# Seven products for eight in a part of each down projection

## The chip, the cores and the metric

The kernel runs on one core of one Trainium2 chip. Its engines work side by side, each through its own queue in order: TensorE (PE) multiplies, VectorE (DVE) and ScalarE (ACT) work element by element, GpSimd (POOL) does small vector work, and SyncE (SP) issues the loads of weights. The metric is the device time of one execution in microseconds (us), as the median over runs. The profile is one further execution, recorded by the hardware profiler.

## The reference, cut to what matters

Two layers work on 256 tokens of width 2048. In each, a mixer (a state-space and gated recurrence in the first, sliding-window attention in the second) is followed by an MLP:

```python
D_MODEL = 2048; SEQ = 256; DEPTH = 2; D_FF = 4 * D_MODEL

def rms_norm(x, gain):
    xf = x.astype(F32)
    y = xf * lax.rsqrt(jnp.mean(xf * xf, axis=-1, keepdims=True) + EPS)
    return (y * gain.astype(F32)).astype(x.dtype)

def squared_relu_mlp(xn, w_up, w_down):
    return jnp.square(jax.nn.relu(xn @ w_up)) @ w_down

def reference(...):
    ...
        h = h + y.astype(h.dtype)
        h = h + squared_relu_mlp(rms_norm(h, mlp_norm[layer]), mlp_w_up[layer], mlp_w_down[layer]).astype(h.dtype)
    return h
```

All is float32. w_up is 2048 x 8192 and w_down 8192 x 2048, in each of the two layers.

## The kernel before

**Products.** A float32 product is made of three products of rounded parts: each operand is split into hi (rounded to the matmul type) and lo (the rest), and hi·hi, hi·lo and lo·hi are added up in PSUM.

**Weights.** All weights of the program are one list of units of 512 KB (`add_units`, lines 79 to 82), used strictly in that order. A down unit is two row tiles of 128 rows by 512 columns, an up unit four row tiles by 256 columns. `emit_dma` (line 92) loads a unit into one of four raw tiles through SP's queue; `emit_split` (line 101) makes hi with a rounding copy on ACT (line 105) and lo with a difference on DVE (line 106), into four buffers each. `advance` (line 110) hands out the next unit and, before that, emits loads up to six units ahead and splits up to three units ahead. A raw tile is free for the unit four places on when its split is done.

**The order on the engines.** The program is written as one stream. A scheduler in the compiler then places the instructions on each engine's queue by its own timeline of them, so that an engine's order can differ from the written one where another instruction was ready first. On the chip each queue runs in the order so found, and semaphores hold an instruction back until its inputs are there.

**The MLP** (`mlp`, line 910) cuts the 8192 hidden columns into four chunks of 2048. `up(c)` makes the activations of a chunk in eight blocks of 256 columns (`ublock`, line 152): after each, ACT and DVE add the two halves of the sum, apply the squared relu and split the result into the pair ch[c] (lines 919 to 925). Here hidden columns lie on partitions and tokens in the free dimension, so the scale of the norm, one number per token, is not applied; its square, `rs2`, multiplies the result of the down projection instead, where tokens lie on partitions (line 935). `down(c)` multiplies a chunk by its 16 row tiles of w_down, in four blocks of 512 output columns, n = 0 to 3, each of eight units (`xblock`, line 168). A unit is 12 products into 512 columns: two token tiles, two row tiles, three parts. Two PSUM accumulators of two banks each alternate (`psA`), and four single banks (`psM`) serve all smaller sums. Each finished block is added into h.

The written order of an MLP is up(0), up(1), down(0), up(2), down(1), up(3), down(2), down(3). After each block of down(3) the next norm's sum of squares and transposes follow (`Norm.block`, line 877), whose last call also computes rs by a power on POOL (line 887). Small side work is kept in a list of generators, `side`, of which `pump` runs some after each unit and `drain` all that is left (lines 126 to 136). The first mixer spreads its own scales over the partitions with a product of ones and a diagonal (`norm0`, line 339), into the tile `rsb`.

Of the kernel before, what the change touches and what calls it, by code (L numbers as in the profile page):

```python
# [8 lines left out]
F32 = mybir.dt.float32  # L9
F32R = mybir.dt.float32r  # L10
# [3 lines left out]
AF = mybir.ActivationFunctionType  # L14
ALU = mybir.AluOpType
AX = mybir.AxisListType

P = 128
T = 256
# [5 lines left out]
SIDE = 1.5  # L25
# [35 lines left out]
def hybrid_kernel(ctx: ExitStack, tc: tile.TileContext, x, even_norm, even_w_in, s5_lambda_re, s5_lambda_im,  # L61
                  s5_log_dt, s5_b_re, s5_b_im, s5_c_re, s5_c_im, s5_d, s5_w_glu, s5_b_glu, hgrn_lower_bound,
                  hgrn_o_norm, even_w_out, odd_norm, odd_w_qkv, q_norm, k_norm, att_sinks, odd_w_out,
                  mlp_norm, mlp_w_up, mlp_w_down, cfd, cmd, out, stop=None):
    nc = tc.nc
    V, S, G, PE = nc.vector, nc.scalar, nc.gpsimd, nc.tensor
    PS = bass.MemoryType.PSUM

    cp = ctx.enter_context(tc.tile_pool(name="cp", bufs=1))
    wp = ctx.enter_context(tc.tile_pool(name="wp", bufs=4))  # L70
    bp = ctx.enter_context(tc.tile_pool(name="bp", bufs=2))
    sp = ctx.enter_context(tc.tile_pool(name="sp", bufs=6))
    psA = ctx.enter_context(tc.tile_pool(name="psA", bufs=2, space=PS))
# [3 lines left out]
    units = []  # L77

    def add_units(W, kts, n0, w=512):
        nk = 1024 // w  # L80
        for i in range(0, len(kts), nk):
            units.append((W, kts[i], n0, nk))

    raws, splits = {}, {}
    ptr = {"dma": 0, "split": 0, "use": 0}

    def pieces(i):

        nk = units[i][3]
        return [slice(k, k + 1) for k in range(nk)] if i == 0 else [slice(0, nk)]  # L90

    def emit_dma(i):
        W, kt, n0, nk = units[i]
        raw = wp.tile([P, nk, 1024 // nk], F32, tag="raw", name="raw", bufs=4)
        src = W[kt * P:(kt + nk) * P, n0:n0 + 1024 // nk].rearrange("(k p) n -> p k n", p=P)
        for ks in pieces(i):
            nc.sync.dma_start(out=raw[:, ks], in_=src[:, ks])
        raws[i] = raw

    def emit_split(i):  # L100
        raw, nk = raws.pop(i), units[i][3]
        hi = wp.tile([P, nk, 1024 // nk], F32R, tag="whi", name="whi")
        lo = wp.tile([P, nk, 1024 // nk], F32R, tag="wlo", name="wlo")
        for ks in pieces(i):
            S.copy(out=hi[:, ks], in_=raw[:, ks])  # L105
            V.tensor_tensor(out=lo[:, ks], in0=raw[:, ks], in1=hi[:, ks].bitcast(F32), op=ALU.subtract)  # L106
        splits[i] = (hi, lo)

    def advance():
        i = ptr["use"]  # L110
        while ptr["dma"] < min(len(units), i + LOOK_DMA + 1) or ptr["split"] < min(len(units), i + LOOK + 1):
            if ptr["dma"] < min(len(units), i + LOOK_DMA + 1) and ptr["dma"] < ptr["split"] + 4:
                emit_dma(ptr["dma"])
                ptr["dma"] += 1
            else:
                emit_split(ptr["split"])
                ptr["split"] += 1
        ptr["use"] += 1
        return splits.pop(i)


    side = []

    def pump(budget):
        while side and budget > 0:
            try:
                budget -= next(side[0])
            except StopIteration:
                side.pop(0)

    def drain(g=None):
        while side and (g is None or g in side):
            pump(1.0)

    def mm(o, a, b, start, stop, **kw):
        PE.matmul(o, a, b, start=start, stop=stop, skip_group_check=True, **kw)  # L136
# [18 lines left out]
    def ublock(XT, kts):  # L155

        acc = psA.tile([P, 2, 2, T], F32, tag="acc", name="acc")
        n = len(kts)
        for i in range(0, n, 4):
            hi, lo = advance()  # L160
            for kk in range(4):
                k = kts[i + kk]
                for m in range(2):
                    mm(acc[:, m], hi[:, kk, m * P:(m + 1) * P], XT.both[:, :, k, :], i + kk == 0, False)
                for m in range(2):
                    mm(acc[:, m, 0], lo[:, kk, m * P:(m + 1) * P], XT.hi[:, k, :], False, i + kk == n - 1)
            pump(SIDE)
        return acc

    def xblock(XT, kts, final=False):  # L170


        n = len(kts)
        if final:
            acc = [pm([P, 512]) for _ in range(2)]
            groups = [(i,) for i in range(0, n - 4, 2)] + [(n - 4, n - 2)]
        else:
            acc = psA.tile([P, 2, 512], F32, tag="acc", name="acc")
            acc = [acc[:, t] for t in range(2)]
            groups = [(i,) for i in range(0, n, 2)]  # L180
        for group in groups:
            w = [advance() for _ in group]
            for t in range(2):
                for i, (hi, lo) in zip(group, w):
                    for kk in range(2):
                        k = kts[i + kk]
                        last = i + kk == n - 1
                        xh, xl = XT.hi[:, k, t * P:(t + 1) * P], XT.lo[:, k, t * P:(t + 1) * P]
                        mm(acc[t], xh, hi[:, kk, :], i + kk == 0, False)
                        mm(acc[t], xh, lo[:, kk, :], False, False)  # L190
                        mm(acc[t], xl, hi[:, kk, :], False, last)
            pump(SIDE)
        return acc

    def pm(shape, dtype=F32):
        return psM.tile(shape, dtype, tag="m", name="m")

    def t4(shape, dtype=F32):
        return sp.tile(shape, dtype, tag="t4", name="t4")

    def new_pair(kind, shape=(P, KD, T)):
        if kind == "x":
            b = bp.tile([P, 2] + list(shape[1:]), F32R, tag="x", name="x", bufs=1)
            pair = Pair(b[:, 0], b[:, 1])
            pair.both = b
            return pair
        bufs = 2
        return Pair(bp.tile(list(shape), F32R, tag=kind + "hi", name=kind + "hi", bufs=bufs),
                    bp.tile(list(shape), F32R, tag=kind + "lo", name=kind + "lo", bufs=bufs))
# [7 lines left out]
    K16, K8 = list(range(16)), list(range(8))  # L217
# [13 lines left out]
    def add_mlp(l):  # L231
        def up(c):
            for n in range(8):
                add_units(mlp_w_up[l], K16, c * 2048 + n * 256, 256)

        def down(c):
            for n in range(4):
                add_units(mlp_w_down[l], [c * 16 + k for k in K16], n * 512)

        up(0)  # L240
        up(1)
        down(0)
        up(2)
        down(1)
        up(3)
        down(2)
        down(3)

    add_mlp(0)
    qkv_cols = [2048, 0, 512, 1024, 1536]  # L250
# [23 lines left out]
    ident = cf[:, 0:128]  # L274
# [59 lines left out]


    rsx = cp.tile([P, 2], F32, name="rsx")
    rsb = cp.tile([P, T], F32, name="rsb")

    def norm0():
        ssx = cp.tile([P, 2, 2], F32, name="ssx")  # L340
# [472 lines left out]
    for i in range(10):  # L813
        if i == 2:
            drain(prep)
        acc = (xblock if i >= 2 and (i - 2) % 4 >= 2 else wblock)(XT0, K16)
        if i < 2:
            drain(n00)
            while "UY" not in st:
                pump(0.1)  # L820
            V.tensor_tensor(out=st["UY"][:, 4 * i:4 * i + 4, :], in0=acc,
                            in1=rsb.unsqueeze(1).to_broadcast([P, 4, T]), op=ALU.mult)
# [5 lines left out]
        hh, j = divmod(i - 2, 4)  # L828
# [4 lines left out]
        for a in range(2):  # L833
            if j < 2:
                d2 = dst[:, a].rearrange("p (m t) -> p m t", m=2)
                V.tensor_tensor(out=d2, in0=acc[:, 2 * a:2 * a + 2, :],
                                in1=rsb.unsqueeze(1).to_broadcast([P, 2, T]), op=ALU.mult)
# [16 lines left out]
    for n in range(2):  # L854
        acc = wblock(yg, K8)
# [3 lines left out]
        for a in range(2):  # L859
# [4 lines left out]
                            op=ALU.subtract)  # L864
    h = cp.tile([P, 2, D], F32, tag="h", name="h", bufs=1)
# [43 lines left out]

    def mlp(norm, nxt):  # L910
        XT = norm.XT
        ch = {}

        def up(c):
            ch[c] = new_pair("c")
            for n in range(8):
                acc = ublock(XT, K16)
                r = t4([P, 2, T])
                S.copy(out=r, in_=acc[:, :, 1])  # L919
                V.tensor_tensor(out=r, in0=acc[:, :, 0], in1=r, op=ALU.add)  # L920
                V.scalar_tensor_tensor(out=r, in0=r, scalar=0.0, in1=r, op0=ALU.max, op1=ALU.mult)  # L921
                ks = slice(2 * n, 2 * n + 2)
                S.copy(out=ch[c].hi[:, ks, :], in_=r)  # L923
                V.tensor_tensor(out=ch[c].lo[:, ks, :], in0=r, in1=ch[c].hi[:, ks, :].bitcast(F32),  # L924
                                op=ALU.subtract)

        def down(c):
            nonlocal nxt
            if c == 3:
                nxt = nxt()  # L930
            for n in range(4):
                acc = xblock(ch[c], K16, c == 3 and n == 3 and nxt.__class__ is Out)
                for t in range(2):
                    cs = slice(n * 512, (n + 1) * 512)
                    V.scalar_tensor_tensor(out=h[:, t, cs], in0=acc[t], scalar=norm.rs2[:, t:t + 1],  # L935
                                           in1=h[:, t, cs], op0=ALU.mult, op1=ALU.add)
                if c == 3:
                    nxt.block(n)

        up(0)  # L940
        up(1)
        down(0)
        up(2)
        down(1)
        up(3)
        down(2)
        down(3)
        return nxt

    def hwait(pi):  # L950
# [144 lines left out]
    acc = xblock(n1.XT, K16)  # L1095
# [57 lines left out]
```

## Time and profile before

| | us |
|---|---|
| median of 3 runs | 2087.06 (2086.74 to 2087.74) |
| profiled execution | 2087.49 |
| its span in the trace | 2085.2 |
| first MLP, from its first up block to the end of its last down block | about 420.6 to 1128 |
| second MLP, from its first up block | about 1375 to the end |
| loads moved in all | 378.86 MB, 182 GB/s over the span |

The two MLPs take two thirds of the span. The profile gives each engine's busy time; its views group instructions by line and form, list who waited for whom, and cut the span into stretches. A product's duration there is its latency from issue to end, and products overlap, so their pace is read from the starts. x counts instructions. PEclk is the clock granted to TensorE as a share of its full speed. "DMA share" is the mean busy share of the 16 DMA engines.

### The profile page before, as it was taken

What the parts mean: (1) busy time and instruction counts of PE and PEld (TensorE: products, weight loads), DVE (VectorE), ACT (ScalarE), POOL (GpSimd) and SP (SyncE); (2) the same over time, 40 slices, a digit from 0 to 9 for tenths busy, and PEclk for the clock granted to TensorE, in tenths of its full rate; (3) what the DMA queues carried; (4) which work ended last, traced back from release to release, by engine and by line L of the source; (5) the groups of instructions that cost most, each with busy time, mean ns of one, the idle gap of its engine ahead of it and who ended that gap; (6) DMA issues with size and microseconds to landing.
All of it is one profiled execution on the core that took longest, in us unless ns stands there. A gap on an engine that the chain in (4) does not pass through costs nothing.

```text
span 2085.2 us, 30704 instructions
## 1 busy us (share of the span) xinstructions
PE 2074.4 (99%) x12208; PEld 1768.5 (85%) x12208; DVE 1320.0 (63%) x1794; ACT 1036.8 (50%) x1385; POOL 38.9 (2%) x38
## 2 busy tenths in 40 slices
PE   9999999999999999999999999999999999999999
PEld 8988988888888888888888888788888888888887
DVE  6799967766655564565555688776565555565544
ACT  5887554554443443444344477664443444344332
POOL 2000000000000000000000110000000000000000
PEclk9999999999999999999999999999999999999999
DMA  8444555566655665665556643456665665665564
GB/s 248 124 149 143 172 163 206 172 182 189 187 190 194 191 191 192 192 191 192 192 190 184 188 146 130 137 178 192 187 188 195 191 190 192 193 190 192 192 202 152
DMA packets 263968, 378.86 MB, mean 182 GB/s; under 512 B 14120, under 2 KB 147792, under 8 KB 263504
## 3 DMA queue, kind: packets, MB, share of 16 engines
q1 hardware_dynamic: 262400, 373.62, 57.1%
q8 instruction: 96, 1.57, 0.3%
q0 software_dynamic: 672, 2.15, 0.3%
q10 hardware_dynamic: 752, 1.12, 0.2%
q14 instruction: 48, 0.39, 0.1%
HBM read 374.75 MB, written 2.10 MB: 181 GB/s over the span
## 4 chain that ended last, share of the span: by engine, by line
PE 96%; ACT 1%; DMA 1%; DVE 1%; issue 0%; SPq 0%; ACTq 0%; DVEq 0%
PE acc L136 90%; PE m L136 4%; DMA raw<-in_even_w_in_dram 1%; PE m L1046 1%; PE m L312 1%; ACT chi L586 0%; ACT whi L105 0%; DVE t L605 0%; PE m L408 0%; DVE wlo L106 0%; PE m L1080 0%; ACT chi L538 0%; DVE t L351 0%; PE m L786 0%; ACT t L574 0%
## 5 line engine op out<-in xcount | busy, mean ns | idle before, releaser
L106 DVE TENSOR_TENSOR wlo<-raw,whi 128x1024 fp32r<-128x1024 f32 (+1 forms) x705 | 860.6, 1222 | 682.8 <-ACT whi L105 682.1
L105 ACT CAST whi<-raw 128x1024 fp32r<-128x1024 f32 (+1 forms) x705 | 740.5, 1051 | 956.4 <-PE acc L136 826.1
L136 PE MATMUL acc<-x,whi 128*128 128x512 f32 (+1 forms) x2816 | 786.2, 366 | 0.2 <-DVE x L316 0.2
L136 PEld LDWEIGHTS acc<-x,wlo 128*128 128x128 f32 x2432 | 457.5, 188 | 91.8 <-DVE wlo L106 0.7
L136 PE MATMUL acc<-x,wlo 128*128 128x256 f32 x2432 | 511.6, 279 | 0.5 <-DVE wlo L106 0.5
L136 PE MATMUL acc<-whi,chi 128*128 128x512 f32 x1248 | 487.5, 391 | 0.0
L136 PE MATMUL acc<-whi,clo 128*128 128x512 f32 x1248 | 486.7, 390 | 0.0
L136 PE MATMUL acc<-wlo,chi 128*128 128x512 f32 x1248 | 486.1, 390 | 0.0
L136 PEld LDWEIGHTS acc<-x,whi 128*128 128x128 f32 x2816 | 432.8, 189 | 2.0 <-issue 0.4
L136 PEld LDWEIGHTS acc<-whi,chi 128*128 128x128 f32 x1248 | 234.3, 188 | 49.1 <-issue 0.8
L136 PEld LDWEIGHTS acc<-whi,clo 128*128 128x128 f32 x1248 | 234.3, 188 | 48.1
L136 PEld LDWEIGHTS acc<-wlo,chi 128*128 128x128 f32 x1248 | 234.3, 188 | 47.9
L136 PE MATMUL acc<-whi,x 128*128 128x512 f32 x576 | 181.4, 393 | 0.0
L136 PEld LDWEIGHTS acc<-whi,x 128*128 128x128 f32 x576 | 107.4, 188 | 22.4 <-issue 0.4
L136 PE MATMUL acc<-wlo,x 128*128 128x512 f32 x288 | 113.4, 394 | 0.0
L136 PEld LDWEIGHTS acc<-wlo,x 128*128 128x128 f32 x288 | 54.1, 188 | 10.9 <-DVE t L605 0.2
L935 DVE SCALAR_TENSOR_TENSOR h<-acc,rs2g,h 128x512 f32<-128x512 f32 x62 | 43.7, 747 | 12.7 <-PE acc L136 12.7
L921 DVE SCALAR_TENSOR_TENSOR t<-t 128x512 f32<-128x512 f32 x64 | 44.3, 693 | 2.2
L920 DVE TENSOR_TENSOR t<-acc,t 128x512 f32<-128x512 f32 x64 | 43.8, 684 | 0.0
L924 DVE TENSOR_TENSOR clo<-t,chi 128x512 fp32r<-128x512 f32 x64 | 43.8, 684 | 0.0
L923 ACT CAST chi<-t 128x512 fp32r<-128x512 f32 x64 | 39.4, 615 | 0.0
L919 ACT COPY t<-acc 128x512 f32<-128x512 f32 x64 | 37.1, 579 | 0.0
(225 smaller groups left out, 1028.0 us busy)
## 6 DMA issues: line engine op xcount, KB each, us to landing
raw<-in_mlp_w_up_dram SPq DMA_DIRECT2D x256, 512.0 KB, 3.7
raw<-in_mlp_w_down_dram SPq DMA_DIRECT2D x256, 512.0 KB, 3.6
raw<-in_even_w_in_dram SPq DMA_DIRECT2D x79, 512.0 KB, 3.8
raw<-in_odd_w_qkv_dram SPq DMA_DIRECT2D x40, 512.0 KB, 3.6
raw<-in_even_w_out_dram SPq DMA_DIRECT2D x32, 512.0 KB, 4.1
raw<-in_odd_w_out_dram SPq DMA_DIRECT2D x32, 512.0 KB, 3.8
raw<-in_s_w_glu_dram SPq DMA_DIRECT2D x8, 512.0 KB, 3.4
xt<-in_x_dram SPq DMA_DIRECT2D x8, 256.0 KB, 7.9
```

The lines of the kernel that those rows point to most:

```text
L105: S.copy(out=hi[:, ks], in_=raw[:, ks])
L106: V.tensor_tensor(out=lo[:, ks], in0=raw[:, ks], in1=hi[:, ks].bitcast(F32), op=ALU.subtract)
L136: PE.matmul(o, a, b, start=start, stop=stop, skip_group_check=True, **kw)
L312: ipe = PE.transpose(ps[:, b, t * P:(t + 1) * P], src[:, t, (a + b) * P:(a + b + 1) * P], ident)
L919: S.copy(out=r, in_=acc[:, :, 1])
L920: V.tensor_tensor(out=r, in0=acc[:, :, 0], in1=r, op=ALU.add)
L921: V.scalar_tensor_tensor(out=r, in0=r, scalar=0.0, in1=r, op0=ALU.max, op1=ALU.mult)
L923: S.copy(out=ch[c].hi[:, ks, :], in_=r)
L924: V.tensor_tensor(out=ch[c].lo[:, ks, :], in0=r, in1=ch[c].hi[:, ks, :].bitcast(F32), op=ALU.subtract)
L935: V.scalar_tensor_tensor(out=h[:, t, cs], in0=acc[t], scalar=norm.rs2[:, t:t + 1], in1=h[:, t, cs], op0=ALU.mult, op1=ALU.add)
L1046: PE.transpose(ps[:, r, a, :], pr[:, 2 * a + r, k * P:(k + 1) * P], ident)
```

## The change

In chunks 0, 1 and 2 of each MLP, for output columns 0 to 1023 (n = 0 and 1) and the first eight of the chunk's 16 row tiles (four pairs, `NS = 4`), the 2 x 2 block of activations (two row tiles by two token tiles) and the 2 x 2 block of weights (two row tiles by two column blocks) are multiplied with seven products instead of eight, in Winograd's form. Each product is still three matmuls into 512 columns. The rest of these chunks, and the whole of chunk 3, multiply as before. The parts:

- *Weights.* A block's weights come in four units instead of two. t1 loads 1024 columns of the first row tile and takes the difference of its halves; t42 loads those of the second, and makes two differences, one of them with t1's; b2 loads the second row tile again, unchanged; b12 loads 512 columns of the first again and subtracts them from b2's. `combine` makes these on DVE, in place in the raw tiles, ahead of the split.
- *Activations.* For the first four up blocks of these chunks, four sums of 128 x 128 tiles are made on DVE, rounded by ACT and split by DVE into the tile `forms`.
- *The norm's scale.* Since these sums mix tokens, the scale is applied to the activations: `row` spreads it over the partitions (two small products, a copy by ACT) once per MLP; the relu's instruction multiplies by it, and ACT squares. The down blocks are then added to h with a plain addition.
- *Sums.* `down_mixed` holds all four single banks of `psM` as a_, c_, e_ and f_. After the t1 and t42 units ACT copies three of them aside; at the end of the b units DVE makes six additions, five of them into h; then the plain units of n = 0 and 1 go on in the same banks.
- *Order.* `down_plan` mixes the block's units with the 16 plain units of n = 2 and 3: for j = 0 and 1, t1, plain, t42, plain, plain; for j = 2 and 3, t1, plain, t42, plain; then for j = 0 and 1, b2, plain, b12, plain; for j = 2 and 3, b2, plain, b12; then eight plain units of n = 0 and 1. The MLP's order becomes up(0), down(0), up(1), down(1) and so on.

```diff
     def emit_dma(i):
-        W, kt, n0, nk = units[i]
+        W, kt, n0, nk, kind = units[i]
         raw = wp.tile([P, nk, 1024 // nk], F32, tag="raw", name="raw", bufs=4)
+        raws[i] = raw
+        if kind is not None:
+
+            w = 512 if kind == "b12" else 1024
+            nc.sync.dma_start(out=raw[:, 0:w // 512], in_=W[kt * P:(kt + 1) * P, n0:n0 + w].rearrange(
+                "p (b n) -> p b n", n=512))
+            return
...
+    def combine(kind, raw):
+
+        def sub(o, a, b):
+            V.tensor_tensor(out=o, in0=a, in1=b, op=ALU.subtract)
+
+        if kind == "t1":
+            sub(raw[:, 1], raw[:, 1], raw[:, 0])
+        elif kind == "t42":
+            sub(raw[:, 0], raw[:, 1], raw[:, 0])
+            sub(raw, held["t1"][:, 1:2].to_broadcast([P, 2, 512]), raw)
+        elif kind == "b12":
+            sub(raw[:, 0], held["b2"][:, 1], raw[:, 0])
+        held[kind] = raw
...
+    NS = 4
+    plain = [(None, n, i) for n in (2, 3) for i in range(8)]
+    down_plan = []
+    for j in range(NS):
+        down_plan += [("t1", 0, j), plain.pop(0), ("t42", 0, j), plain.pop(0)]
+        if j < 2:
+            down_plan.append(plain.pop(0))
+    for j in range(NS):
+        down_plan += [("b2", 0, j), plain.pop(0), ("b12", 0, j)]
+        if plain and j < 2:
+            down_plan.append(plain.pop(0))
+    down_plan += plain + [(None, n, i) for n in (0, 1) for i in range(NS, 8)]
...
+        def row():
+
+            dg = t4([P, 3, P])
+            V.memset(dg[:, 2, :], 1.0)
+            for t in range(2):
+                V.tensor_scalar(out=dg[:, t, :], in0=ident, scalar1=norm.rs[:, t:t + 1], scalar2=None, op0=ALU.mult)
+            yield 1.5
+            ps = pm([P, 2, P])
+            for t in range(2):
+                mm(ps[:, t, :], dg[:, 2, :], dg[:, t, :], True, True)
+            S.copy(out=rst, in_=ps.rearrange("p t n -> p (t n)"))
+            yield 0
...
-                V.scalar_tensor_tensor(out=r, in0=r, scalar=0.0, in1=r, op0=ALU.max, op1=ALU.mult)
+                V.scalar_tensor_tensor(out=r, in0=r, scalar=0.0, in1=rst.unsqueeze(1).to_broadcast([P, 2, T]),
+                                       op0=ALU.max, op1=ALU.mult)
+                S.activation(out=r, in_=r, func=AF.Square)
...
+                if c < 3 and n < NS:
+                    a11, a21, a12, a22 = [r[:, k, t * P:(t + 1) * P] for k in range(2) for t in range(2)]
+                    s_ = t4([P, 4, P])
+                    for o, a, b, op in ((0, a21, a22, ALU.add), (1, a11, s_[:, 0], ALU.subtract),
+                                        (2, a11, a21, ALU.subtract), (3, a12, s_[:, 1], ALU.add)):
+                        V.tensor_tensor(out=s_[:, o], in0=a, in1=b, op=op)
+                    fh, fl = forms[c][:, 0, n], forms[c][:, 1, n]
+                    S.copy(out=fh, in_=s_)
+                    V.tensor_tensor(out=fl, in0=s_, in1=fh.bitcast(F32), op=ALU.subtract)
...
+                if kind == "t1":
+                    triple(a_, *whole(2 * j, 0), *w[0], j == 0, False)
+                    triple(c_, *form(j, 0), *w[1], j == 0, False)
+                elif kind == "t42":
+                    triple(f_, *whole(2 * j + 1, 1), *w[0], j == 0, False)
+                    triple(e_, *form(j, 1), *w[1], j == 0, False)
+                    if j == NS - 1:
+                        S.copy(out=s1, in_=a_)
+                        S.copy(out=s5, in_=c_)
+                        S.copy(out=s6, in_=e_)
+                elif kind == "b2":
+                    triple(a_, *whole(2 * j + 1, 0), *w[0], False, False)
+                    triple(c_, *form(j, 3), *w[1], False, False)
+                elif kind == "b12":
+                    triple(e_, *form(j, 2), *w[0], False, j == NS - 1)
+                    if j == NS - 1:
+                        V.tensor_tensor(out=v, in0=e_, in1=s1, op=ALU.add)
+                        hadd(0, 1, s1)
+                        hadd(0, 1, s6)
+                        hadd(1, 0, v)
+                        hadd(1, 1, v)
+                        hadd(1, 1, s5)
...
-        up(0)
-        up(1)
-        down(0)
-        up(2)
-        down(1)
-        up(3)
-        down(2)
-        down(3)
+        for c in range(4):
+            up(c)
+            down(c)
```

More of the change, by code (lines that the diff above doesn't have):

```diff
@@ L81, in add_units @@
         for i in range(0, len(kts), nk):
-            units.append((W, kts[i], n0, nk))
+            units.append((W, kts[i], n0, nk, None))
     raws, splits = {}, {}
@@ L97, in emit_dma @@
             nc.sync.dma_start(out=raw[:, ks], in_=src[:, ks])
-        raws[i] = raw
+    held = {}
+    def combine(kind, raw):
[9 more added lines that the diff above has]
+        held[kind] = raw
     def emit_split(i):
-        raw, nk = raws.pop(i), units[i][3]
+        raw, nk, kind = raws.pop(i), units[i][3], units[i][4]
+        if kind is not None:
+            combine(kind, raw)
         hi = wp.tile([P, nk, 1024 // nk], F32R, tag="whi", name="whi")
         lo = wp.tile([P, nk, 1024 // nk], F32R, tag="wlo", name="wlo")
-        for ks in pieces(i):
+        for ks in ([slice(0, 1)] if kind == "b12" else pieces(i)):
             S.copy(out=hi[:, ks], in_=raw[:, ks])
@@ L236, in down @@
         def down(c):
-            for n in range(4):
-                add_units(mlp_w_down[l], [c * 16 + k for k in K16], n * 512)
-        up(0)
-        up(1)
-        down(0)
-        up(2)
-        down(1)
-        up(3)
-        down(2)
-        down(3)
+            if c == 3:
+                for n in range(4):
+                    add_units(mlp_w_down[l], [c * 16 + k for k in K16], n * 512)
+                return
+            for kind, n, i in down_plan:
+                if kind is None:
+                    add_units(mlp_w_down[l], [c * 16 + 2 * i, c * 16 + 2 * i + 1], n * 512)
+                else:
+                    units.append((mlp_w_down[l], c * 16 + 2 * i + (kind in ("t42", "b2")),
+                                  512 if kind == "b12" else 0, 2, kind))
+        for c in range(4):
[13 more added lines that the diff above has]
+    down_plan += plain + [(None, n, i) for n in (0, 1) for i in range(NS, 8)]
     add_mlp(0)
@@ L336, in hybrid_kernel @@
     rsx = cp.tile([P, 2], F32, name="rsx")
-    rsb = cp.tile([P, T], F32, name="rsb")
+    rsb = cp.tile([P, T], F32, tag="rsb", name="rsb", bufs=1)
     def norm0():
@@ L911, in mlp @@
         XT = norm.XT
-        ch = {}
+        ch, forms = {}, {}
+        rst = cp.tile([P, T], F32, tag="rsb", name="rst", bufs=1)
+        def row():
[9 more added lines that the diff above has]
+            yield 0
+        side.append(row())
         def up(c):
             ch[c] = new_pair("c")
+            if c < 3:
+                forms[c] = sp.tile([P, 2, NS, 4, P], F32R, tag="q1", name="forms", bufs=1)
             for n in range(8):
                 acc = ublock(XT, K16)
+                drain()
                 r = t4([P, 2, T])
@@ new lines, in hadd, with down_mixed, triple, whole @@
+        def hadd(t, n, o):
+            cs = slice(n * 512, (n + 1) * 512)
+            V.tensor_tensor(out=h[:, t, cs], in0=o, in1=h[:, t, cs], op=ALU.add)
+        def down_mixed(c):
+            X, F = ch[c], forms[c]
+            a_, c_, e_, f_ = [pm([P, 512]) for _ in range(4)]
+            half = {0: (a_, f_), 1: (c_, e_)}
+            s15, s6v = t4([P, 2, 512]), t4([P, 2, 512])
+            s1, s5, s6, v = s15[:, 0], s15[:, 1], s6v[:, 0], s6v[:, 1]
+            accs = {}
+            def triple(o, fh, fl, wh, wl, start, stop):
+                mm(o, fh, wh, start, False)
+                mm(o, fh, wl, False, False)
+                mm(o, fl, wh, False, stop)
+            def whole(k, t):
+                return X.hi[:, k, t * P:(t + 1) * P], X.lo[:, k, t * P:(t + 1) * P]
+            def form(j, i):
+                return F[:, 0, j, i], F[:, 1, j, i]
+            for kind, n, j in down_plan:
+                hi, lo = advance()
+                w = [(hi[:, b], lo[:, b]) for b in range(2)]
+                if kind == "t1":
[20 more added lines that the diff above has]
+                        hadd(1, 1, s5)
+                else:
+                    if n not in accs:
+                        if n > 1:
+                            acc = psA.tile([P, 2, 512], F32, tag="acc", name="acc")
+                            accs[n] = [acc[:, t] for t in range(2)]
+                        else:
+                            accs[n] = half[n]
+                    for t in range(2):
+                        for kk in range(2):
+                            first = j + kk == 0 if n > 1 else n == 1 and t == 1 and j == NS and kk == 0
+                            triple(accs[n][t], *whole(2 * j + kk, t), *w[kk], first, j == 7 and kk == 1)
+                    if j == 7:
+                        for t in range(2):
+                            hadd(t, n, accs[n][t])
+                    pump(SIDE)
@@ L927, in down @@
         def down(c):
             nonlocal nxt
-            if c == 3:
-                nxt = nxt()
+            if c < 3:
+                return down_mixed(c)
+            nxt = nxt()
             for n in range(4):
-                acc = xblock(ch[c], K16, c == 3 and n == 3 and nxt.__class__ is Out)
+                acc = xblock(ch[c], K16, n == 3 and nxt.__class__ is Out)
                 for t in range(2):
[L934 to L947, printed above, removed]
+                    hadd(t, n, acc[t])
+                nxt.block(n)
+        for c in range(4):
+            up(c)
+            down(c)
         return nxt
```

## The prediction

> **What bounds the kernel now.** I read the busy shares first, then the chain that ended last, then TensorE's own waits.
>
> ```profile
> span 2085.2 us, 30704 instructions
> ...
> PE 2074.4 (99%) x12208; PEld 1768.5 (85%) x12208; DVE 1320.0 (63%) x1794; ACT 1036.8 (50%) x1385; POOL 38.9 (2%) x38
> ...
> PE 96%; ACT 1%; DMA 1%; DVE 1%; issue 0%; SPq 0%; ACTq 0%; DVEq 0%
> ```
>
> TensorE (PE) is 99% busy and is 96% of the chain; VectorE (DVE) has 63%, ScalarE (ACT) 50%. The list of who waited for whom has less than 7 us of PE waits in all, and only these two touch a projection:
>
> ```profile
> PE acc L136 <- DVE wlo L106: 0.5, 1, 0.5
> ...
> PE acc L136 <- DVE x L316: 0.2, 1, 0.2
> ```
>
> So a product taken away is time taken away, as long as its replacement does not make PE wait. Next, the views of one down chunk (first row), one up chunk (second), and the first and last of 24 neighbouring products in a down chunk:
>
> ```profile
> core 0: us, PE busy (x) PEld busy (x) DVE busy (x) ACT busy (x) POOL busy (x), PEclk, DMA share, GB/s
> 600.62:688.40 87.78, 87.78 (x391) 72.75 (x390) 46.26 (x43) 35.11 (x35) 0.00 (x0) 1.00 0.59 193
> 688.40:776.80 88.40, 88.40 (x509) 77.12 (x508) 52.59 (x54) 40.27 (x46) 0.00 (x0) 1.00 0.62 190
> ...
> 600.62 0.40 PE L136 MATMUL acc<-whi,chi 128*128 128x512 f32 x1
> ...
> 605.84 0.39 PE L136 MATMUL acc<-whi,clo 128*128 128x512 f32 x1
> ```
>
> The 0.39 us of a product is its latency; the pace is (605.84 - 600.62) / 23 = 0.227 us at a granted clock of 1.00. A plain unit of 12 products is 2.72 us, and 32 of them make the 87 us chunk. DVE has 41 us to spare in a down chunk.
>
> **The change part by part.** *Removed.* One 2x2x2 block (two row tiles, two token tiles, two column blocks) was 8 x 3 = 24 products and becomes 7 x 3 = 21. With 4 blocks in 3 chunks of 2 layers, 72 products go: 72 x 0.227 = **-16.3 us**. All lies on the path.
>
> *Added on PE.* Once per MLP two small products spread the row of scales. The same form ran once at the start (first row):
>
> ```profile
> 40.50 0.61 PE L136 MATMUL m<-t 128*128 128x128 f32 x4
> ...
> L357 DVE MEMSET t<- x1: 165/165/165, 32.0 to 32.0; 128x128 f32 x1
> ...
> L1035 DVE TENSOR_SCALAR clo<-clo,dn 128x128 f32<-128x128 f32 x24 | 5.4, 281 | 0.2
> ...
> 420.57 0.71 PE L136 MATMUL acc<-x,whi 128*128 128x512 f32 x2
> ...
> 424.07 0.70 POOL L887 TENSOR_TENSOR rsg<-rsg,nhalf 128x2 f32<-128x2 f32 x1 [43.82 <-DVE rs2g L886]
> ...
> 429.35 0.48 DVE L316 SCALAR_TENSOR_TENSOR x<-m,vec,x 128x256 fp32r<-128x256 f32 x1
> ```
>
> That is 2 x 0.61 = **+1.2 us**. It waits for POOL's power (done at 424.8) and 0.17 + 2 x 0.28 = 0.73 us of DVE. Behind the waiting product stand the first up block's third and fourth units. The last slice of normalised tokens ends at 429.8, and would end near 430.6; its tile is used in the fourth unit, which starts three units of 88.4 / 32 = 2.76 us after 420.6 and takes its four row tiles 0.69 us apart, so the last near 430.9. I cost this wait at nothing; without that slack it is 1 us a time, so 0 to 2 us.
>
> *Added in the up chunks.* A Square on ACT per block, and for half of the blocks of six chunks four sums of 128 columns, a rounding copy and a difference:
>
> ```profile
> L921 DVE SCALAR_TENSOR_TENSOR t<-t 128x512 f32<-128x512 f32 x64 | 44.3, 693 | 2.2
> ...
> L924 DVE TENSOR_TENSOR clo<-t,chi 128x512 fp32r<-128x512 f32 x64 | 43.8, 684 | 0.0
> ...
> L923 ACT CAST chi<-t 128x512 fp32r<-128x512 f32 x64 | 39.4, 615 | 0.0
> L919 ACT COPY t<-acc 128x512 f32<-128x512 f32 x64 | 37.1, 579 | 0.0
> ...
> L880 ACT ACTIVATE t<-h 128x512 f32<-128x512 f32 x24 | 14.9, 625 | 0.0
> ...
> L666 DVE TENSOR_TENSOR t<-t 128x128 f32<-128x128 f32 x1 | 0.3, 285 | 0.0
> ```
>
> Per chunk that is 4 x (4 x 0.285 + 0.684) = 7.3 us on DVE, 52.6 to 60 of 88.4 us, and 8 x 0.625 + 4 x 0.615 = 7.5 us on ACT, 40 to 48. PE hides it: **0**. The cover that goes would be the blocks' 11 us each.
>
> *Moved.* Chunk c is now contracted right after it is made. Its last two row tiles come from the last up block, whose after-work (0.58 + 0.68 + 0.69 + 0.63 + 0.62 + 0.68 = 3.9 us) is needed only by the fourteenth unit of the chunk (n=2, i=7), some 25 us later: **0**. The mixed sums hold PSUM tiles that no side work of an MLP's first three chunks asks for.
>
> *Added in the mixed chunks.* This decides. The costs, by form:
>
> ```profile
> L106 DVE TENSOR_TENSOR wlo<-raw,whi 128x1024 fp32r<-128x1024 f32 x703 | 859.2, 1223 | 678.4 <-ACT whi L105 677.7
> L105 ACT CAST whi<-raw 128x1024 fp32r<-128x1024 f32 x703 | 739.2, 1052 | 954.4 <-PE acc L136 826.1 <-issue 99.9 <-DMA raw<-in_even_w_in_dram 7.6
> ...
> L905 DVE TENSOR_TENSOR h<-acc,h 128x512 f32<-128x512 f32 x48 | 30.8, 685 | 8.4 <-PE acc L136 8.4
> ```
>
> DVE per unit, all in us: plain 1.22; t1 0.68 + 1.22 = 1.90; t42 0.68 + 1.22 + 1.22 = 3.12; b2 1.22; b12 0.68 + 0.68 = 1.36. PE: plain 2.72, t1, t42 and b2 1.36 each, b12 0.68. The plan then gives:
> - first half, j=0 and 1 (t1, t42, three plain): DVE 8.68, PE 10.89 each;
> - first half, j=2 and 3 (t1, t42, two plain): DVE 7.46, PE 8.16 each;
> - second half, j=0 and 1: DVE 5.02, PE 7.48; j=2 and 3: DVE 3.80, PE 4.76.
>
> To the first half come the tail of the last up block (2.06) and two additions into h (1.37): DVE 35.7 of PE's 38.1 us, 94%. In its j=2 and 3 it is 16.3 of 16.3 us with the additions. Then it falls to 72%, and the final six adds (4.1 us) meet eight plain units with 12 us free. So by sums DVE still fits; what it loses in order, it loses with four units of finished weights ahead (four buffers). Two stretches of before show what a full DVE costs PE (columns as in the windows above), with PE's only wait of 104 to 260 us:
>
> ```profile
> 156.00:208.00 52.00, 52.00 (x424) 45.08 (x422) 51.18 (x100) 37.90 (x41) 0.00 (x0) 1.00 0.49 146
> 208.00:260.00 52.00, 52.00 (x651) 47.70 (x644) 49.28 (x85) 29.77 (x35) 1.27 (x2) 1.00 0.58 169
> ...
> PE m L136 <- DVE t L605: 0.5, 2, 0.3
> ```
>
> DVE was 98% busy for 52 us and PE lost next to nothing. There much of DVE's work could be put off, here none can. The lower bound of the stall is thus 0, the upper is DVE in strict program order, where it also stands idle for each rounding copy (1.05 us) between a combination and its difference: t1 2.95, t42 4.17, so j=2 and 3 take 9.56 for PE's 8.16. Late by 2 x 1.40 + 1.37 + 2.06, less 2 x 0.10 spare in j=0 and 1: 6.0 us a chunk. But the order is not the program's:
>
> ```profile
> 602.87 0.69 DVE L921 SCALAR_TENSOR_TENSOR t<-t 128x512 f32<-128x512 f32 x1
> 603.83 0.61 ACT L923 CAST chi<-t 128x512 fp32r<-128x512 f32 x1
> 603.95 1.22 DVE L106 TENSOR_TENSOR wlo<-raw,whi 128x1024 fp32r<-128x1024 f32 x1 [0.39 <-ACT whi L105]
> 605.10 0.69 DVE L924 TENSOR_TENSOR clo<-t,chi 128x512 fp32r<-128x512 f32 x1
> ```
>
> A later weight difference was put into the gap that ACT's copy leaves. So I take 1.0 us a chunk, nearer to the stretches of before than to 6.0: 6 x 1.0 = **+6.0 us** (0 to 36).
>
> Sum on the profiled execution: 2087.49 - 16.3 + 1.2 + 6.0 = 2078.4 (its span 2085.2 would be 2076.1, with 2.3 around it). The median of the runs lies 0.4 lower, so **2078.0**.
>
> **The loads.** Half of the block's rows are read twice and slots are held: t1's raw tile stays until t42 has been combined, b2's until b12 has.
>
> ```profile
> raw<-in_mlp_w_down_dram SPq DMA_DIRECT2D x256, 512.0 KB, 3.6
> ...
> SPq L97 <- DVE wlo L106: 1583.8, 647, 9.6
> ...
> q1 hardware_dynamic: 3799, 5.53, 96.0%
> ...
> raw<-in_even_w_in_dram SPq DMA_DIRECT2D x7, 512.0 KB, 8.5
> ```
>
> The first row is the usual load of a unit, 3.6 us from issue to landing; the second says that SP's queue waits for DVE to free a slot, and behind it every later load waits; the last two are 4 to 22 us of the span, where the 16 DMA engines are 96% busy and the same load takes 8.5 us. In j=2 and 3 four units (2.10 MB) in 8.16 us are 257 GB/s, at the rate of the down chunk (0.59 for 193) a share of 0.79; at the end of the second half 1.31 MB in 4.76 us, 0.84. The next t1 needs 3.6 + 0.68 + 1.05 + 1.22 = 6.6 us from the freed slot to its use, of 8.2 us of PE: 1.6 us of slack. I cost it at nothing; it starts to cost at a landing of 5.2 us.
>
> The Trainium skill, "DMA: Bandwidth & Descriptors", section "Latency and other measured facts", speaks against this: it gives reads of HBM 0.2 us on average and 2 us at high load as the main part of a transfer's fixed cost. By it a landing would be 3.6 + 1.8 = 5.4 us, an estimate, 0.2 over the slack, and the sum 2 to 3 us higher. The trace agrees in direction (3.6 against 8.5 us); no row shows a share of 0.8 in this pattern.
>
> **The rivals.**
> 1. *DVE's order makes it the bound in j=2 and 3 of the first half.* For it: 16.3 of 16.3 us, and combination, copy and difference are a chain across two engines. Against it: the filled gap at 603.95. Price up to 6.0 us a chunk; with half of the lead absorbing 2 us, 4.0: 2087.1 - 15.1 + 24 = 2096 (2084 to 2108). It turns the sign at 15.1 / 6 = 2.5 us a chunk. This is the slower side.
> 2. *Loads land too late* because slots are held. For it: the 8.5 us; against it: shares stay below 0.85. At a landing of 6.2 us two t1 a chunk are 1.0 us late: 2087.1 - 15.1 + 12 = 2084; at 8.5 us, 3.3 x 2 x 6 = 40: 2112.
> 3. *No stall at all.* For it: the 52 us of full DVE. 2087.1 - 15.1 = 2072.
> 4. *The change does not do what it says:* PE's pace of the new products is slower by what they save, as in changes of PSUM bank at every third product. Against it: the up products change their accumulator at each step, and an up chunk's 256 x (512 + 256) columns in 88.4 us are 0.230 us per 512. With the rest of the sum, 2087.1 + 7.2 = 2094.
>
> **How the numbers follow.** Forecast (0.3 to 2 us of stall a chunk, 2074 to 2084) 0.43; rival 1 0.26; rival 2 0.12; rival 3 0.14; rival 4 0.03; the rest 0.02. About 0.2%, 4.2 us, is what a measurement here can tell from no change. Below 2082.9 lie most of the forecast (0.39), rival 3 and a third of rival 2: 0.57. Within 0.2%, up to 2091.2, lie 0.04 of the forecast, 0.09 of rival 1 and 0.06 of rival 2: 0.19. Slower: the rest, 0.24. The range goes from just under no stall, 2071.5, to 2100, where rival 1 costs (2100 - 2072) / 6 = 4.7 us a chunk, most of the way to its bound of 6.0.
>
> **What would show it.** PE's products into 512 columns should be 72 fewer at an unchanged pace, and its waits for wlo and whi should lie in the first half of the mixed chunks, at 6 us in all. Waits of more than 15 us there, with DVE busy throughout, are rival 1; with ACT or DVE waiting for raw, rival 2. Up chunks should stay at 88.4 us. A plain tail of eight units slower than 21.8 us, or a wait at the first up block of over 1 us, would be a cost that I have set at nothing.

## The result: slower, and the profile after

The changed kernel takes 2111.44 us (median of 4 runs, 2109.52 to 2112.92), against 2087.4 us for the kernel before in the same comparison: a ratio of 1.0114, 95% interval 1.0097 to 1.0132. The forecast was 2078.0, with a range from 2071.5 to 2100. The page of the changed kernel begins so (busy time, share of the span and instructions of each engine, and the chain that ended last):

```profile
span 2110.3 us, 31236 instructions
...
PE 2075.3 (98%) x12144; PEld 1754.9 (83%) x12144; DVE 1481.7 (70%) x2100; ACT 1136.9 (54%) x1541; POOL 38.8 (2%) x38
...
PE 78%; DMA 11%; DVE 7%; issue 2%; ACT 2%; SPq 0%; DVEq 0%; ACTq 0%
PE acc L160 65%; PE m L160 12%; DMA raw<-in_mlp_w_down_dram 10%; DVE wlo L130 4%; DVE raw L111 2%; ACT whi L129 1%; PE m L353 1%; PE m L1174 1%; DMA xt<-in_x_dram 0%; DVE t L646 0%; DVE h L1000 0%; PE m L449 0%; DVE clo L986 0%; PE m L1208 0%; ACT chi L627 0%
```

TensorE has 64 instructions fewer: 72 products went and 8 came with the two rows of scales. But it is only 78% of the chain now, where it was 96%; loads of w_down are 10% of it and VectorE 7%. The list of who waited for whom says where they bite:

```profile
ACT whi L129 <- DMA raw<-in_mlp_w_down_dram: 120.5, 88, 3.7
DVE raw L111 <- DMA raw<-in_mlp_w_down_dram: 110.6, 71, 4.2
...
ACT whi L129 <- DVE raw L111: 74.0, 45, 3.7
...
PEld m L160 <- ACT whi L129: 25.4, 27, 1.5
...
PEld m L160 <- DVE wlo L130: 15.4, 16, 2.6
PE m L160 <- ACT whi L129: 14.7, 23, 1.1
```

Line 111 is the sums of weights, 129 and 130 are the split into hi and lo. In the kernel before, neither ACT nor DVE waited for a load of w_down at all. The starts of line 979, the first copy after each up block, give the time of one mixed chunk with the up block that follows it. (Each figure is the distance between the last such copy of a chunk and the first of the next.)

| us per mixed chunk and one up block | six chunks | mean |
|---|---|---|
| changed kernel, four raw tiles | 104.3, 101.7, 102.5, 101.1, 101.2, 101.4 | 102.0 |
| with a second buffer (first experiment below) | 95.5, 95.5, 95.5, 96.2, 95.5, 95.5 | 95.6 |

An up block is 11.1 us, so the second row leaves 84.4 us for a mixed chunk, and 372 products at 0.227 us are 84.4 us: next to nothing is lost in it. The changed kernel loses 6 x 6.4 = 38 us in the same six places; its up blocks, and the stretch between the two MLPs, are as long as in that other kernel. So the 16 us were saved, and about 40 us of waiting (2110.3 less 2085.2 - 16.3 + 1.2) came in. By the page, 24 of them are idle time of TensorE (2110.3 - 2075.3 = 35.0 us, where it was 2085.2 - 2074.4 = 10.8), and 16 stand in its busy time (2075.3 us, where 2074.4 - 16.3 + 1.2 = 2059.3 would be due): products that started late while the one before was still under way, or ran at the lower clock of the last section.

How such a wait arises is shown by the chain that ended last, from 526 us on, in the third and fourth steps (j = 2 and 3) of the first mixed chunk's first half (start, duration, what; a DMA row runs from the issue of the load to its landing):

```profile
526.12 5.30 DMA raw<-in_mlp_w_down_dram
531.42 0.03 issue
531.45 0.02 DVEq L111
531.47 0.04 issue
531.51 0.69 DVE raw L111
532.21 0.07 DVE wlo L130
532.28 0.98 issue
533.26 1.23 DVE raw L111
...
534.59 1.06 ACT whi L129
...
535.67 1.24 DVE wlo L130
536.92 4.79 DMA raw<-in_mlp_w_down_dram
...
546.13 5.89 DMA raw<-in_mlp_w_down_dram
```

TensorE does not occur in it. A raw tile is given to t42's load at 526.12 us. The load lands 5.3 us later, VectorE makes the two sums (with another unit's difference between them), ACT rounds, VectorE makes the difference, and at 536.92 the same tile is given to the next step's t42. The round is 10.8 us, and TensorE needs 36 x 0.227 = 8.2 us for the step's four units. With four tiles for four units, every tile must make its round within a step. The loop of tiles sets the pace, 2.6 us too long in this step. The round is no fixed size, since it holds waits in the queues: the next one, to 546.13, takes 9.2 us. By the starts of the loads the first of the two takes 10.3 to 11.0 us in the six chunks and the second 9.1 to 9.6.

### The profile page after: what moved, and what is told of

Read it like the earlier page. It is cut to its first block, busy times and chain, and to the rows that moved or that the text cites. A ratio compares the mean times of both kernels' runs of the same rounds, so it can differ in the third digit from the quotient of the medians.

```text
span 2110.3 us, 31236 instructions
## 1 busy us (share of the span) xinstructions
PE 2075.3 (98%) x12144; PEld 1754.9 (83%) x12144; DVE 1481.7 (70%) x2100; ACT 1136.9 (54%) x1541; POOL 38.8 (2%) x38
## 4 chain that ended last, share of the span: by engine, by line
PE 78%; DMA 11%; DVE 7%; issue 2%; ACT 2%; SPq 0%; DVEq 0%; ACTq 0%
PE acc L160 65%; PE m L160 12%; DMA raw<-in_mlp_w_down_dram 10%; DVE wlo L130 4%; DVE raw L111 2%; ACT whi L129 1%; PE m L353 1%; PE m L1174 1%; DMA xt<-in_x_dram 0%; DVE t L646 0%; DVE h L1000 0%; PE m L449 0%; DVE clo L986 0%; PE m L1208 0%; ACT chi L627 0%
## 5 line engine op out<-in xcount | busy, mean ns | idle before, releaser
L160 PE MATMUL acc<-whi,chi 128*128 128x512 f32 x864 | 338.9, 392 | 0.1
L160 PE MATMUL acc<-wlo,chi 128*128 128x512 f32 x864 | 338.1, 392 | 0.0
L160 PE MATMUL acc<-whi,clo 128*128 128x512 f32 x864 | 338.0, 392 | 0.0
L160 PEld LDWEIGHTS acc<-whi,chi 128*128 128x128 f32 x864 | 162.3, 188 | 35.5 <-ACT whi L129 1.6
L160 PEld LDWEIGHTS acc<-whi,clo 128*128 128x128 f32 x864 | 162.5, 188 | 33.6
L111 DVE TENSOR_TENSOR raw<-raw 128x512 f32<-128x512 f32 (+1 forms) x96 | 79.1, 824 | 110.9 <-DMA raw<-in_mlp_w_down_dram 110.6
L160 PE MATMUL m<-whi,chi 128*128 128x512 f32 x296 | 112.1, 398 | 14.7 <-ACT whi L129 14.7
L160 PE MATMUL m<-wlo,chi 128*128 128x512 f32 x296 | 116.9, 395 | 9.6 <-DVE wlo L130 9.4
L160 PE MATMUL m<-whi,clo 128*128 128x512 f32 x296 | 115.5, 390 | 0.0
L160 PE MATMUL m<-whi,forms 128*128 128x512 f32 x192 | 75.3, 392 | 0.0
```

Of the source, the lines that this page charges most:

```text
L111: V.tensor_tensor(out=o, in0=a, in1=b, op=ALU.subtract)
```

## The experiments

Two theories at first. **S**: the four raw tiles set the pace, each tied up from the issue of its load until its sums and its split are done. **V**: VectorE's amount of work and its fixed order set it (rival 1 of the prediction). Later came **L**, that loads are written too few units ahead, and **O**, that the sums stand in the wrong place in VectorE's queue. The numbers of tiles in the headings and in the expectations are those of the written program; how many the chip had in use is said where it differs. All times are medians.

### Seven tiles, as written

The mixed units are loaded into the buffer `t4`, which the mixed chunks use little, beside the four raw tiles for the plain units, and the look-ahead of loads is 9 instead of 6.

```diff
-LOOK_DMA = 6
+LOOK_DMA = 9
...
-        raw = wp.tile([P, nk, 1024 // nk], F32, tag="raw", name="raw", bufs=4)
+        raw = (t4([P, 2, 512]) if kind is not None else
+               wp.tile([P, nk, 1024 // nk], F32, tag="raw", name="raw", bufs=4))
...
-            if ptr["dma"] < min(len(units), i + LOOK_DMA + 1) and ptr["dma"] < ptr["split"] + 4:
+            if ptr["dma"] < min(len(units), i + LOOK_DMA + 1) and room():
```

`room` counts the tiles of each kind that loads have been written for and that are not yet free, and lets three mixed ones be written ahead. This bounds only the written order. `t4` itself has six tiles (the pool `sp`, `bufs=6`), the scheduler may place a load earlier than it is written, and in this kernel's trace up to six mixed units are loaded or being loaded and not yet split. On the chip it is a second buffer of six tiles, not three more tiles.

> The mixed units are loaded into three tiles of another buffer, beside the four raw tiles, and loads may be emitted up to nine units ahead. Theory S (four raw tiles, each tied up from the issue of its load until its sums and its split are done, set the pace in the mixed stretch): the waits for loads go and the time falls to 2075 to 2085 us. Theory V (VectorE's amount of work and its fixed order set the pace): it stays at 2105 to 2112 us, with VectorE waiting for ScalarE or for nothing instead of for loads.

Measured: 2072.38 us, ratio to before 0.9926 (0.991 to 0.9943). Less than both ends of what S gave, and 39 us under the changed kernel. In the list of waits, VectorE still stands waiting for loads (t is now the tile), but TensorE and its weight loads hardly wait for hi or lo any more (1.1 us is the largest such entry, where it was 25.4):

```profile
DVE t L112 <- DMA t<-in_mlp_w_down_dram: 63.4, 45, 4.1
...
ACT whi L130 <- DMA t<-in_mlp_w_down_dram: 1.9, 1, 1.9
```

The loads themselves are no faster, as the list of DMA issues shows (KB each, median us to landing):

```profile
raw<-in_mlp_w_down_dram SPq DMA_DIRECT2D x208, 512.0 KB, 4.0
t<-in_mlp_w_down_dram SPq DMA_DIRECT2D x72, 512.0 KB, 5.2
```

They only start early enough. V falls. Whether the number of tiles did it, or that mixed and plain units no longer take turns in one ring, this run does not tell.

### No tile held for a later unit

```diff
-            sub(raw, held["t1"][:, 1:2].to_broadcast([P, 2, 512]), raw)
+            sub(raw, raw[:, 1:2].to_broadcast([P, 2, 512]), raw)
...
-            sub(raw[:, 0], held["b2"][:, 1], raw[:, 0])
+            sub(raw[:, 0], raw[:, 0], raw[:, 0])
```

> The sums of weights are made from the unit's own tile alone, in as many instructions of the same size, so that no tile is held for a later unit; the weights so made are not those of the seven products. Theory S, if the holding is what ties the tiles up: 2085 to 2098 us. Theory S, if the length of load, sum and split is: 2100 to 2110 us. Theory V: within 4 us of the changed kernel's 2111.

Measured: 2102.07 us. The hold alone is 9 of the 39 us (5 to 11 over this run's executions); the rest of the round (load, sums, split) carries the larger part.

### No sums of weights

```diff
-            combine(kind, raw)
+            pass
```

> The sums of weights are left out; loads, splits and products are all there, on plain weights. Theory S: a tile is then tied up for a load and a split, 6.5 us against 8.2 us of TensorE for four units, and the time is 2072 to 2078 us. Theory V: the same, since VectorE loses 79 us of work. Over 2090 us would say that the loads' own rate is the bound.

Measured: 2071.36 us. The loads are all there, twice-read rows included, and cost nothing: their rate is not the bound. Without sums and hold a round fits into a step even with four tiles. (This run takes the waiting sums off VectorE's queue too, so it does not tell S from O.)

### The change without the seven products

```diff
-            if c < 3:
-                return down_mixed(c)
-            nxt = nxt()
+            if c == 3:
+                nxt = nxt()
```

The units of weights are the plain ones in all chunks.

> All down chunks are multiplied with eight products as before, with the other parts of the change in place: the order of chunks, the scale on the activations, the squares, the sums of activations. Both theories: 2087 to 2090 us, 1.2 us over before for the scale's row. Over 2095 us would put a part of the loss outside the mixed chunks.

Measured: 2088.03 us against 2086.9, ratio 1.0005 (0.9996 to 1.0014). The 1.1 us are close to the 1.2 set for the rows of scales, and no more than the interval allows for no change at all; order, squares and sums of activations cost nothing that shows. So the loss belongs to the mixed chunks.

### Four, five and six tiles, as written

The kernel above has four tiles for plain units and lets three mixed loads be written ahead. Here it is two and two, two and three, two and four (mixed first), all with the look-ahead of 9. The plain tiles are a buffer of that size. The mixed ones are again the six tiles of `t4`.

> As the seven-tile kernel, with its deeper look-ahead and its two kinds of tiles, but two tiles for mixed units and two for plain ones in place of three and four: four in all, as in the changed kernel. Theory S: the gain goes with the number of tiles, so 2100 to 2150 us, in the mixed chunks and in the up chunks too, which then have two. Theory L (the deeper look-ahead or the other order it brings was what helped): 2072 to 2085 us.

> Two tiles for mixed units and three for plain ones. Theory S: between four tiles and six, 2080 to 2105 us. Theory L: 2072 to 2085 us.

> Two tiles for mixed units and four for plain ones. Theory S, if only the number counts: 2072 to 2082 us. If the mixed units are what lacks tiles, since t1 and t42 or b2 and b12 fill both: 2085 to 2105 us.

| mixed loads written ahead + plain tiles | us | ratio to before |
|---|---|---|
| 2 + 2 | 2250.54 | 1.0788 (1.077 to 1.0806) |
| 2 + 3 | 2073.03 | 0.9933 (0.9918 to 0.9948) |
| 2 + 4 | 2071.87 | 0.9928 (0.9913 to 0.9943) |
| 3 + 4 | 2072.38 | 0.9926 (0.991 to 0.9943) |

The first number did not bind on the chip: in all four runs up to six mixed units are loaded, or being loaded, and not yet split. In the run "2 + 3", for example:

```profile
499.48 0.94 SPq L100 DMA_DIRECT2D t<-in_mlp_w_down_dram  x2
510.87 2.91 SPq L100 DMA_DIRECT2D t<-in_mlp_w_down_dram  x3
...
511.46 1.22 DVE L131 TENSOR_TENSOR wlo<-t,whi 128x1024 fp32r<-128x1024 f32 x1
519.36 1.22 DVE L131 TENSOR_TENSOR wlo<-t,whi 128x1024 fp32r<-128x1024 f32 x1
```

The two differences finish the split of the mixed unit before these five and of the first of them, so from 514 to 519 us five mixed tiles are in use where two were meant. These runs therefore do not say that five tiles are enough; with `t4`'s six, the chip had up to nine there. What they show is the second number. With two plain tiles the kernel is far slower, and with three the loss is gone, which agrees with S: the tiles set the pace.

With two and two, the profiled execution is 152 us longer than the changed kernel's. About 66 us of it are in the up blocks (12.3 us each instead of 11.1), whose units are all plain, 29 in the six mixed chunks with the up block behind each (105.1 to 108.1 us, some 5 us more than the changed kernel's, of which the slower up block may have a part), and the rest in the other stretches, which have plain units alone. In that kernel ACT's waits for loads of w_down are nearly three times those of the changed one:

```profile
ACT whi L130 <- DMA raw<-in_mlp_w_down_dram: 335.5, 153, 6.6
```

So neither the deeper look-ahead nor the two kinds of tiles help by themselves.

### More work for VectorE, with seven tiles

```diff
             sub(raw, held["t1"][:, 1:2].to_broadcast([P, 2, 512]), raw)
+            for _ in range(2):
+                sub(raw, held["t1"][:, 1:2].to_broadcast([P, 2, 512]), raw)
```

> Seven tiles, and the second sum of every t42 three times instead of once: 24 x 2 x 1.22 = 59 us more on VectorE, all in the first halves, where VectorE then has 9.9 us a step for TensorE's 8.2 at j = 2 and 3 and 11.1 for 10.9 at j = 0 and 1. The weights so made are others. If VectorE was far from its bound with seven tiles: up to 2076 us. If it was at the edge, as the sums of the prediction have it: 2.1 x 2 + 0.2 x 2 = 4 to 6 us a chunk less the lead, 2085 to 2105 us.

The expectation errs in a detail: taken three times, the difference gives what it gives once, so the weights are the same. Measured: 2071.3 us, no more than with seven tiles alone, with this much more on VectorE (1481.7 us in the changed kernel):

```profile
PE 2059.2 (99%) x12144; PEld 1756.2 (85%) x12144; DVE 1534.2 (74%) x2148; ACT 1137.6 (55%) x1541; POOL 38.9 (2%) x38
```

VectorE's amount of work was not the bound. My sum of 9.9 us of VectorE for 8.2 us of TensorE in two steps (1.7 us over, not the 2.1 of the expectation) did not come out as a stall. I can only argue why: the surplus is less than 4 us in a chunk, finished weights lie up to four units ahead, and instructions that follow at once take a little less than their durations (two of 1.22 us took 2.35 us together in the changed kernel).

### Look-ahead alone

```diff
-LOOK_DMA = 6
+LOOK_DMA = 9
```

> The changed kernel with its four raw tiles, and loads written up to nine units ahead instead of six. Theory S (number of tiles): 2105 to 2116 us, as the changed kernel, since a load still waits for one of four tiles. Theory L (how far ahead loads are written): 2072 to 2085 us.

Measured: 2107.86 us (2106.52 to 2111.33). L falls; 3.6 us between the medians are all that it gives, and the executions of the two kernels overlap.

### The written order on VectorE, with four tiles and with seven

In the changed kernel VectorE waited 110.6 us for loads with a sum at the head of its queue. Here a sum must come after the difference of the unit before, as written.

```diff
-            V.tensor_tensor(out=o, in0=a, in1=b, op=ALU.subtract)
+            with tc.issue_after(last_lo[0].ins):
+                V.tensor_tensor(out=o, in0=a, in1=b, op=ALU.subtract)
```

> The changed kernel with four raw tiles, but VectorE must take the sums of a unit behind the difference of the unit before, as written, so that no sum that waits for its load stands ahead of a difference that is ready. Theory S: within 8 us of the changed kernel's 2111. Theory O (the scheduler's place for the sums, ahead of work that was ready, is the loss): 2075 to 2095 us. Rival 1 of the prediction (the written order costs up to 6 us a chunk): over 2120 us.

> The seven-tile kernel with the sums in the written order on VectorE. This prices rival 1 of the prediction by itself, with loads early enough: by its sum 4 to 6 us a chunk, 2096 to 2108 us. Theory S: with tiles enough, VectorE's order matters little, 2071 to 2080 us.

Measured: 2092.78 us with four tiles, 2076.2 with seven. With four, VectorE's waits for loads are gone, and ACT's waits for the sums have doubled from 74.0 us:

```profile
ACT whi L130 <- DVE raw L112: 138.3, 63, 4.2
...
ACT whi L130 <- DMA raw<-in_mlp_w_down_dram: 85.4, 80, 3.5
...
DVE raw L112 <- DMA raw<-in_mlp_w_down_dram: 2.5, 5, 0.9
```

This lies between the theories, and both have a part. A sum that waits at the head of the queue holds back a difference that is ready, and that difference would free a tile and let a load start. In the changed kernel's trace:

```profile
528.51 1.06 ACT L129 CAST whi<-raw 128x1024 fp32r<-128x1024 f32 x1 [1.27 <-DVE raw L111]
...
531.51 0.69 DVE L111 TENSOR_TENSOR raw<-raw 128x512 f32<-128x512 f32 x1 [2.04 <-DMA raw<-in_mlp_w_down_dram]
532.12 1.22 DVE L130 TENSOR_TENSOR wlo<-raw,whi 128x1024 fp32r<-128x1024 f32 x1
```

The rounded part of t1 is there at 529.57, but VectorE makes the difference only at 532.12, behind a sum of t42 for which it waited 2.04 us. The written order takes away 18.7 of the 39 us at four tiles. The other 20 us stay with four tiles in any order tried. With the second buffer the scheduler's own order is the better one, by 3.8 us; in the written order VectorE's differences wait longer for ACT to round (511.7 us in the list of waits, against 451.6).

### Five pairs of row tiles

Three plain tiles, three mixed loads written ahead (into `t4`'s six tiles), and `NS = 5`, with the plain units spread anew over the longer mixed stretch.

> Three tiles for mixed units and three for plain ones (six), and five of the eight pairs of row tiles in seven products instead of four: 18 more products go, 18 x 0.227 = 4.1 us. Theory S, with tiles enough: 2066 to 2070 us. If VectorE or the loads bind again in the longer mixed stretch: over 2072 us.

Measured: 2069.1 us, ratio 0.9918 (0.9903 to 0.9933), the lowest median of all. Against 2071.9 of the run "2 + 4", with four pairs, it is 2.8 us, of the 4.1 that the products are worth; so small a difference lies under the 4.2 us that the prediction gives as the least that can be told apart.

## Why the prediction was wrong

**The step that failed is the loads, costed at nothing.** I had the hold of t1's and b2's tiles and the queue behind them, and set 6.6 us from a freed slot to its use against 8.2 us of TensorE: "1.6 us of slack", to be used up at a landing of 5.2 us. Two things in it were wrong. The sum began at the freed slot, as if a slot were free one step ahead; it is itself freed late, by the step before. What must fit into a step is the whole round of a tile, with what stands in the queues between: 10.8 us in the trace. And landings were taken at 3.6 us. In the chain above they are 5.30, 4.79 and 5.89 us, with a median of 4.2 over all full loads of w_down:

```profile
raw<-in_mlp_w_down_dram SPq DMA_DIRECT2D x280, 512.0 KB, 4.2
```

The cost was 39 us, not 0, and rival 2, which had a chance of 0.12, was the one that came, by its sign (ACT and VectorE waiting for raw) and by its cause (held slots, late loads). Its prices were not right. At landings of 6.2 us it would have given 2084; it counted two late loads in a chunk, where ACT and VectorE wait some 26 times in each (88 and 71 times in all six). Its other price, 2112 us at landings of 8.5 us, meets the measured time by luck: in the mixed stretches no load took longer than 6.9 us, and the median is 4.3 to 4.6. And 18.7 of the 39 us hang on the place of the sums in VectorE's queue, which it did not name.

**TensorE's terms were right.** The -16.3 us and the +1.2 us give 2072 us, and with the second buffer, in the scheduler's order, the kernel takes 2071.3 to 2073.0. That was rival 3. The rows' wait, the sums of activations, the squares and the order of the chunks cost nothing, as the run without the seven products shows.

**VectorE's term was 0 instead of 6 us,** where tiles do not bind, and rival 1 fell with it. There the written order costs 3.8 us in all, 0.7 us a chunk in the distances of the copies (96.2 against 95.5), where I had set up to 6.0 a chunk. The stretch of before in which VectorE was 98% busy without harm was the right row to go by, and more weight should have been on it. With four tiles I had the order the wrong way round: I took the written one as the worst case and the scheduler's as the cure, and the written one was 18.7 us the better. A sum waiting at the head of VectorE's queue delays the release of tiles, and this I had not seen.

**The rule weighed there** (the Trainium skill, "DMA: Bandwidth & Descriptors", section "Latency and other measured facts": a read of HBM costs more at high load) pointed the right way. By it I had 2 to 3 us. The trace agrees that loads landed later (4.2 against 3.6 us in the middle), but no run shows that the HBM's latency is why. With the second buffer the mixed units' loads landed at 5.2 us and cost nothing, so a late landing alone is not the loss; by these runs it costs where no tile is free early enough.

What stays open: how many tiles are enough, since every run with a second buffer had up to six tiles for the mixed units; whether more tiles in one ring would do as well, or mixed and plain units must be kept apart; and what a lower landing time would give with four tiles.

## What to carry to other kernels

When a change lengthens what a buffer goes through (a hold, one more pass in place, a re-read), add up the buffer's whole round, from the issue of its load to its release, with the waits in the queues between, and divide by the number of buffers: that is the pace it allows, and it is to be set against the pace of the consumer. Here it was 9.2 to 10.8 us over four tiles against 8.2 us for four units. Busy shares do not show it: VectorE was at 70% and the DMA queue of the weights at 59%, and each stood waiting for the other. A scheduler's order that puts a waiting instruction at the head of a queue makes such a round longer. Here the other order was worth 18.7 us, and the second buffer 39. And a limit written into the program may not hold after the scheduler: count in the trace how many tiles are in use before a result is put down to their number.

## What the runs showed of the hardware

One long wait of TensorE cost more than its length. In the changed kernel, 5 us windows from 570 us (span, busy time of PE with its instructions, granted clock, DMA share, GB/s), and single products behind TensorE's longest wait there, with their durations:

```profile
570.00:575.00 5.00, 5.00 (x23) 1.00 0.63 204
575.00:580.00 5.00, 2.72 (x7) 0.80 0.29 99
580.00:585.00 5.00, 5.00 (x20) 0.86 0.94 311
...
577.94 0.77 PE L160 MATMUL m<-wlo,chi 128*128 128x512 f32 x1 [2.28 <-DVE wlo L130]
578.50 0.63 PE L160 MATMUL m<-whi,clo 128*128 128x512 f32 x1
578.93 0.63 PE L160 MATMUL m<-wlo,forms 128*128 128x512 f32 x1
...
581.47 0.39 PE L160 MATMUL acc<-whi,clo 128*128 128x512 f32 x1
```

After 2.28 us without work the granted clock fell (0.80 and 0.86 in the two windows), and products started 0.43 us apart, where it is 0.227: eight of them, from 577.94 to 581.47, took 3.5 us. The Trainium skill, "TensorE: Matmul & The Clock Gate", section "Part 1: The HAM clock gate", gives a half clock after an idle window of about 3.4 us; here a gap of 2.3 us was followed by it. This once cost 3.5 - 8 x 0.227 = 1.7 us on top of the wait.
